# Pool's queue carries the statistics and outputs of a dilated attention, and keys and values of the next pair are loaded in parts

## The chip, the cores and the metric

The kernel runs on one core of one Trainium2 chip. The metric is device time in microseconds (us). It was timed three times before the change, with a median of 3201.4 us. One more execution was profiled, and every row below is of that one.

## What is computed

The reference is a trunk of two decoder layers over 2048 positions of 1024 channels, in float32. The change touches the mixer of the second layer only, a causal dilated attention with three branches of 16 heads:

```
DILATED_CONFIGS = ((128, 1), (512, 4), (2048, 16))
...
def dilated_mixture(q, k, v):
    branches = [dilated_window_branch(q, k, v, d, w // d) for (w, d) in DILATED_CONFIGS]
    big_m = branches[0][1]
    for _, m_i, _ in branches[1:]:
        big_m = jnp.maximum(big_m, m_i)
    num = 0.0
    den = 0.0
    for o_i, m_i, l_i in branches:
        w_i = l_i * jnp.exp(m_i - big_m)
        num = num + w_i * o_i.astype(jnp.float32)
        den = den + w_i
    return (num / den).astype(v.dtype)
```

Each branch has, for every head and query, an output, a row maximum m and a row sum l. The outputs are added with weights made from m and l, then multiplied by a gate, silu of a fourth projection.

## The kernel before

Queries, keys, values and gates of the second layer are written to DRAM by the projections. The function `dilated` reads them back. It handles the 16 heads as eight pairs p = 0 to 7, a pair in four chunks c of 512 queries, and a chunk as four units: a half of the chunk (`half`) in each of two branches `br` (the first two dilations share one). A unit multiplies queries with keys (L1268, tile `s_ps`), adds a mask and takes the row minimum on DVE (L1276), takes the exponential with its row sum on ACT (L1278), transposes the result on PE (`flip`, L709) with copies back from PSUM (L713, tile `pt`), and multiplies with the values (L1309, tile `o_ps`).

What joins the branches is `merge`. Its steps hang behind the last unit of a pair and are issued one per unit while the next pair runs:

- `rows` transposes the statistics of a pair and writes them to DRAM (ACT copy L1337 into `rt`, then four DMAs `std<-rt`).
- `columns` reads them back in another layout (nine DMAs `W<-std`). The first five bring what the first step of `weights` needs, the last four what L1358 needs.
- `weights` makes the weights on DVE (L1355 `mm`, L1356, L1358, L1359 to L1364) and ACT (L1357).
- `expand` spreads them over partitions on Pool (L1370, tile `X`), and `chunk` multiplies each output with its weight (PE L1378, DVE L1379), adds the two branches and multiplies with the gate on Pool (L1385, L1386), and writes the result to DRAM (`og`).

Pairs 0 to 6 merge all four chunks at once (n = 4). Pair 7 merges each chunk by itself, since the output projection that follows waits for it. The projection (`out_proj`, PE L618) loads the outputs back; its first four row tiles and one weight tile are loaded from Pool's queue.

A DMA is issued by the engine whose queue `queue[0]` holds: SP (`nc.sync`) everywhere in `dilated` apart from the first loads, which Pool (`PO`) issues. Each engine runs its instructions in order, and a DMA that waits for a semaphore holds everything behind it in its queue. The order of an engine's instructions is set when the program is built, by a planner that moves an instruction to where it expects it to be ready. A load that is issued early in the code therefore stands in SP's queue behind other loads and waits only for its buffer.

Keys take four buffers (two pairs), values four (two pairs of two branches), queries three, gates four.

Of the kernel before, what the change touches and what calls it, by code (L numbers as in the profile page):

```python
# [8 lines left out]
F32 = mybir.dt.float32  # L9
F32R = mybir.dt.float32r  # L10
# [8 lines left out]
S, D = 2048, 1024  # L19
# [64 lines left out]
def trunk(ctx: ExitStack, tc: tile.TileContext, A, out):  # L84
    nc = tc.nc
    V, SC, PO, TE = nc.vector, nc.scalar, nc.gpsimd, nc.tensor

    queue = [nc.sync]
    QA = PO

    def dma(o, i):
        if o.dtype == F32R:
            o = o.bitcast(F32)
        if i.dtype == F32R:
            i = i.bitcast(F32)
        return queue[0].dma_start(o, i)  # L96
# [7 lines left out]
    def dap(t, off, ap):  # L104
        return bass.AP(tensor=t.tensor, offset=t.offset + off, ap=ap)

    def pool(es, name, bufs=1, space=None, side=None):
        kw = {"space": space} if space is not None else {}
        if side is not None:
            kw["side"] = side  # L110
        return es.enter_context(tc.tile_pool(name=name, bufs=bufs, reuse_waits="tile", **kw))
# [6 lines left out]
    k1 = dram.tile([2, 16, 64, S], F32R, name="k1")  # L118
    v_d = [dram.tile([S, 1024], F32, name=f"v_{l}") for l in range(2)]
    sg_d = [dram.tile([8, 128, S], F32, name=f"sg_{l}") for l in range(2)]  # L120
# [448 lines left out]
    for u in range(4):  # L569
# [3 lines left out]
                 lambda part, j, c, u=u: qk0[2 * u + j][part, :, 512 * c:512 * c + 512])  # L573
# [30 lines left out]
    def split_wo(raw, where):  # L604

        for c in (0, 512):
            hi, lo = where[:, c:c + 512], where[:, D + c:D + c + 512]
            SC.copy(hi, raw[:, c:c + 512])
            V.tensor_tensor(lo, raw[:, c:c + 512], hi.bitcast(F32), OP.subtract)
# [536 lines left out]
    def dilated():  # L1146
        es = ExitStack()
        kp = pool(wo_es, "kp1")
        ap = pool(es, "dl")
        ap2 = pool(es, "dl2")  # L1150
# [3 lines left out]
        wo = []  # L1154
        keys, queries, values, gates, stats, outs, Os, raws = {}, {}, {}, {}, {}, {}, {}, []

        def load_k(p, cuts=(0, 1024, 2048)):

            keys[p] = K = [kp.tile([128, S], F32R, tag="K", name="K", bufs=4) for _ in range(2)]
            for a, b in zip(cuts[:-1], cuts[1:]):  # L1160
                for k in range(2):
                    dma(K[k][:, a:b], dap(k1, (16 * k + 2 * p) * 64 * S + a, [[S, 128], [1, b - a]]))

        def load_q(p, c, parts=(0, 4)):

            queries[p, c] = Q = kp.tile([128, 4, 512], F32R, tag="Q", name="Q", bufs=3)
            for a, b in zip(parts[:-1], parts[1:]):
                dma(Q[:, a:b], dap(q1, (128 * p * 16 + 4 * c + a) * 512, [[16 * 512, 128], [512, b - a], [1, 512]]))
# [13 lines left out]
        band = kp.tile([128, 768], F32, name="band")  # L1182
        bands = band[:, 0:512], band[:, 512:768]
        queue[0] = QA
        load_k(0, (0, 512))
        load_q(0, 0, (0, 2, 4))
        dma(band, A["cst"][:, C_MB:C_MB + 768])
        for k in range(2):
# [46 lines left out]
        def unit(p, c, br, half):  # L1235
# [6 lines left out]
            def start():  # L1242
                if half == 0 and br == 0:
                    g = 4 * p + c + 1
                    if g < 32:
                        load_q(g // 4, g % 4)
                    if c == 0:
                        stats[p] = ap.tile([128, 4, 2, 2, 2, 4], F32, tag="st", name="st", bufs=2)
                        if p < 7:
                            load_k(p + 1)  # L1250

            def scores(js):
                Kh, Kl = keys[p]
# [29 lines left out]
            def turn(s):  # L1283
                if s == 0:
                    if p == 7 and br == 0 and c > 0:
                        (out_weights if half == 0 else lambda e: split_wo(raws[e // 2][:, e % 2], wo[e]))(c - 1)
                    if p < 7 and (c, half) == (1, 0):
                        load_v(p + 1, br)
                engs = []
                for _ in range(2):  # L1290
                    count[0] += 1
                    engs.append(SC if count[0] % 3 == 0 else V)
                where.update(zip(steps[s], flip(ap, aps, [box["P"][:, hh, j, o:o + 128] for hh, j, o, kc in steps[s]],
                                                engs, DPT_BUFS)))
# [30 lines left out]
        def merge(p, c0, n):  # L1325

            box = {}
            R = 8 * n
            sd = st_d[p + c0]

            def rows():

                ps = x_bank("x_ps")
                TE.transpose(ps[0:4 * R, 0:128],
                             stats[p][:, c0:c0 + n].rearrange("p c x b h t -> p (c x b h t)"), ident)
                rt = ap2.tile([128, 128], F32, tag="rt", name="rt", bufs=2)
                SC.copy(rt[0:4 * R], ps[0:4 * R, 0:128])  # L1337
                for c in range(n):
                    dma(dap(sd, c * 512, [[n * 512, 8], [128, 4], [1, 128]]), rt[32 * c:32 * c + 32])

            def columns():

                box["W"] = W = ap2.tile([128, 2, 2, 128], F32, tag="W", name="W", bufs=1)
                dma(W[0:R, :, 0], dap(sd, 0, [[128, R], [2 * R * 128, 2], [1, 128]]))
                for k in range(2):
                    for t in range(4):
                        dma(W[0:R, k, 1, 32 * t:32 * t + 32],
                            dap(sd, (2 * k + 1) * R * 128 + 128 * t, [[512, 2 * n], [32, 4], [1, 32]]))

            def weights():  # L1350
                W = box["W"][0:R]
                m, l = W[:, 0], W[:, 1]
                mm = ap2.tile([128, 128], F32, tag="mm", name="mm", bufs=1)[0:R]
                E = ap2.tile([128, 2, 128], F32, tag="E", name="E", bufs=1)[0:R]
                V.tensor_tensor(mm, m[:, 0], m[:, 1], OP.min)  # L1355
                V.tensor_tensor(E, mm[:, None, :].to_broadcast([R, 2, 128]), m, OP.subtract)  # L1356
                SC.activation(E, E, AF.Exp)  # L1357
                V.tensor_tensor(l, l, E, OP.mult)  # L1358
                V.tensor_tensor(mm, l[:, 0], l[:, 1], OP.add)  # L1359
                V.reciprocal(mm, mm)  # L1360
                V.tensor_tensor(E, E, mm[:, None, :].to_broadcast([R, 2, 128]), OP.mult)
                ws = [ap2.tile([128, 2, 128], F32R, tag=f"w{k}", name=f"w{k}", bufs=1)[0:R] for k in range(2)]
                V.tensor_copy(ws[0], E)
                V.tensor_tensor(ws[1], E, ws[0].bitcast(F32), OP.subtract)  # L1364
                box["w"] = ws

            def expand(br):

                for k in range(2):
                    PO.tensor_tensor(X[64 * br + 32 * k:64 * br + 32 * k + R].rearrange("p (r y) -> p r y", r=4),  # L1370
                                     box["w"][k][:, br, None, :].bitcast(F32).to_broadcast([R, 4, 128]),
                                     cc[0:R, C_M4:C_M4 + 4, None].to_broadcast([R, 4, 128]), OP.mult)

            def chunk(c, br):
                o = outs[p, br, c]
                bc = x_bank("bc_ps")
                bs = slice(64 * br, 64 * br + 64)
                TE.matmul(bc, sels[2 + c if n == 4 else 6][bs], X[bs], start=True, stop=True)  # L1378
                V.tensor_tensor(o, bc, o, OP.mult)  # L1379
                if br == 0:  # L1380
                    gates[p, c] = ap2.tile([128, 512], F32, tag="sg", name="sg", bufs=4)
                    dma(gates[p, c], sg_d[1][p, :, 512 * c:512 * c + 512])
                    return
                eng = V if (p, c) == (7, 3) else PO
                eng.tensor_tensor(o, o, outs[p, 0, c], OP.add)  # L1385
                eng.tensor_tensor(o, o, gates[p, c], OP.mult)  # L1386
                dma(og_d[1][c][p], o)

            if p < 6:
                fs = [rows, columns, None, None, weights, lambda: expand(0), lambda: expand(1), None]  # L1390
                fs += [lambda c=c, br=br: chunk(c, br) for c in range(4) for br in range(2)]
            else:
                fs = [rows, columns] + [None] * (c0 < 3) + [weights, lambda: (expand(0), expand(1))]
                fs += [lambda c=c: (chunk(c, 0), chunk(c, 1)) for c in range(c0, c0 + n)]
            return [(i + 1, f) for i, f in enumerate(fs) if f]
# [16 lines left out]
    DLEAD, DPT_BUFS, OR_BUFS = 4, 6, 11  # L1412
    wo_es = ExitStack()
    wo_tiles = dilated()

    out_proj(1, None, *wo_tiles)
# [51 lines left out]
```

## Time and profile before

| what | value |
|---|---|
| three timed executions | 3199.12, 3201.4, 3201.77 us |
| the profiled execution, its own time | 3197.35 us |
| its span, first to last instruction | 3195.4 us |
| PE busy | 3052.8 us (96%) |
| DVE, ACT, Pool busy | 1567.6, 1281.4, 511.2 us |
| mean granted TensorE clock | 0.976 |
| bytes moved by DMA | 415.27 MB, 130 GB/s |

The profiled execution is 1.95 us longer than its span, and 4.05 us under the median. The dilated attention runs from about 2499 us to about 2997 us of the span, with the output projection behind it. A busy time is the time in which an engine had an instruction under way; a matmul at half clock is busy for twice as long. The granted clock is a share of 2.4 GHz.

### The profile page before, as it was taken

What the parts mean: (1) busy time and instruction counts of PE and PEld (TensorE: products, weight loads), DVE (VectorE), ACT (ScalarE), POOL (GpSimd) and SP (SyncE); (2) the same over time, 40 slices, a digit from 0 to 9 for tenths busy, and PEclk for the clock granted to TensorE, in tenths of its full rate; (3) what the DMA queues carried; (4) which work ended last, traced back from release to release, by engine and by line L of the source; (5) the groups of instructions that cost most, each with busy time, mean ns of one, the idle gap of its engine ahead of it and who ended that gap; (6) DMA issues with size and microseconds to landing.
All of it is one profiled execution on the core that took longest, in us unless ns stands there. A gap on an engine that the chain in (4) does not pass through costs nothing. (4 is left out here: it accounts for less than half of the span.)

```text
span 3195.4 us, 60888 instructions
## 1 busy us (share of the span) xinstructions
PE 3052.8 (96%) x24252; PEld 2498.1 (78%) x24252; DVE 1567.6 (49%) x4176; ACT 1281.4 (40%) x2954; POOL 511.2 (16%) x495
## 2 busy tenths in 40 slices
PE   7999999999999999999999999999999988988898
PEld 5978888987777777677778999888888777777687
DVE  6443421000777778888654411411100578878643
ACT  4411111111766665655542221111111677776321
POOL 3200100001332310000033101320000012213321
PEclk8999999999999999999999999999999999998899
DMA  7255553215323222222253323675322755654252
GB/s 256 74 189 194 156 154 104 73 61 183 111 92 118 82 68 74 73 69 67 80 187 107 126 81 118 205 216 157 115 82 94 214 165 180 196 167 146 91 175 97
DMA packets 272309, 415.27 MB, mean 130 GB/s; under 512 B 28172, under 2 KB 155788, under 8 KB 267032
## 3 DMA queue, kind: packets, MB, share of 16 engines
q1 hardware_dynamic: 268712, 399.58, 38.9%
q0 software_dynamic: 3312, 11.80, 1.2%
q8 instruction: 190, 3.11, 0.4%
q14 instruction: 95, 0.78, 0.1%
HBM read 259.23 MB, written 152.05 MB: 129 GB/s over the span
## 5 line engine op out<-in xcount | busy, mean ns | idle before, releaser
L246 PE MATMUL pj<-hl,wh 128*128 128x512 f32 x1536 | 389.6, 396 | 0.0
L246 PE MATMUL pj<-hh,wh 128*128 128x512 f32 x1536 | 389.3, 395 | 0.0
L246 PE MATMUL pj<-hh,wl 128*128 128x512 f32 x1536 | 388.3, 395 | 0.0
L834 PE MATMUL s_ps<-K,Q 64*128 64x512 f32 (+2 forms) x1920 | 335.5, 392 | 19.1 <-DVE P L843 15.1
L246 PEld LDWEIGHTS pj<-hl,wh 128*128 128x128 f32 x1536 | 289.1, 188 | 68.6 <-issue 0.2
L854 ACT ACTIVATE P<-P,m 128x1664 f32<-128x1664 f32 (+15 forms) x256 | 306.7, 1200 | 88.0 <-DVE m L849 87.8
L246 PEld LDWEIGHTS pj<-hh,wl 128*128 128x128 f32 x1536 | 288.5, 188 | 68.3 <-issue 0.2
L246 PEld LDWEIGHTS pj<-hh,wh 128*128 128x128 f32 x1536 | 288.2, 188 | 68.4 <-issue 1.0
L709 PE MATMUL t_ps<-cc,P 64*128 64x64 f32 x5536 | 306.4, 234 | 29.5 <-DVE pt L713 19.1
L709 PEld LDWEIGHTS t_ps<-cc,P 64*128 64x128 f32 x5536 | 239.9, 142 | 107.5 <-issue 57.2
L923 PEld LDWEIGHTS o_ps<-pt,v 128*64 128x64 f32 (+1 forms) x3264 | 248.9, 156 | 85.8 <-issue 52.3
L923 PE MATMUL o_ps<-pt,v 128*64 128x128 f32 (+1 forms) x3264 | 311.9, 284 | 2.9 <-ACT pt L713 2.7
L1278 ACT ACTIVATE P<-P,st 128x256 f32<-128x256 f32 (+3 forms) x512 | 267.0, 524 | 89.5 <-DVE st L1276 88.2
L231 DVE TENSOR_TENSOR wl<-w,wh 128x512 fp32r<-128x512 f32 (+1 forms) x128 | 84.8, 705 | 406.7 <-ACT wh L230 406.7
L713 ACT COPY pt<-t_ps 128x512 f32<-128x512 f32 (+7 forms) x448 | 213.5, 496 | 164.7 <-PE t_ps L709 152.2
L713 DVE COPY pt<-t_ps 128x512 f32<-128x512 f32 (+5 forms) x384 | 229.6, 608 | 75.7 <-PE t_ps L709 64.2
L1276 DVE CUSTOM_DVE_ANT_0 P<-s_ps,band 128x256 f32<-128x256 f32 (+3 forms) x512 | 204.4, 446 | 98.6 <-PE s_ps L1268 95.3
L834 PEld LDWEIGHTS s_ps<-K,Q 64*128 64x128 f32 x1920 | 200.5, 191 | 61.1 <-DVE P L843 25.3
L1268 PE MATMUL s_ps<-K,Q 64*128 64x256 f32 (+2 forms) x1536 | 192.4, 337 | 24.7 <-DVE st L1276 23.6
L267 ACT ACTIVATE hi<-pj 128x512 fp32r<-128x512 f32 x80 | 47.9, 599 | 348.8 <-PE pj L246 327.7
L268 DVE SCALAR_TENSOR_TENSOR lo<-pj,hi 128x512 fp32r<-128x512 f32 x80 | 55.2, 690 | 246.0 <-ACT hi L267 233.8
L840 DVE CUSTOM_DVE_ANT_0 P<-s_ps,F 128x512 f32<-128x512 f32 (+1 forms) x192 | 121.4, 670 | 109.9 <-PE s_ps L834 109.1
(245 smaller groups left out, 4475.5 us busy)
## 6 DMA issues: line engine op xcount, KB each, us to landing
Q<-q SPq DMA_DIRECT2D x31, 1024.0 KB
ada<-ada_w SPq DMA_DIRECT2D x96, 256.0 KB
sg<-t2k SPq DMA_DIRECT2D x64, 256.0 KB
xt<-x SPq DMA_DIRECT2D x32, 512.0 KB
w<-w SPq DMA_DIRECT2D x64, 256.0 KB
q<-yb SPq DMA_DIRECT2D x64, 256.0 KB
x<-x SPq DMA_DIRECT2D x28, 512.0 KB
w<-w0b SPq DMA_DIRECT2D x56, 256.0 KB
```

The costliest lines, as they stand in the source:

```text
L231: V.tensor_tensor(wl[:, 2 * q:2 * q + 2, :n], w[:, :, :n], wh[:, 2 * q:2 * q + 2, :n].bitcast(F32), OP.subtract)
L246: TE.matmul(ps, a[:, d, 128 * j:128 * j + 128], b[:, d, :], start=n == 0, stop=n == 23)
L268: V.scalar_tensor_tensor(lo, src, scale, hi.bitcast(F32), OP.mult, OP.subtract)
L709: TE.transpose(ps[k][:, n], b[rs], ident[rs, rs])
L713: last_flip[eng is SC] = f(pt[:, :len(blocks), 64 * k:64 * k + 64], ps[k][:, :len(blocks)])
L834: TE.matmul(ps[j][:, :n], queries[p, i // 4][hs, a, qs], keys[p][b][hs, c0:c0 + n], start=first, stop=a == 1)
L840: V.tensor_tensor_reduce(P[:, c0:c0 + n], ps[j][:, :n], forgets[p][j][:, c0:c0 + n], 1.0, 3.0e38, OP.add, OP.min, m)
L854: SC.activation(P, P, AF.Exp, bias=lows[j], scale=-1.0, accum_out=lt[:, j, col:col + 1])
L923: TE.matmul(o[:, cs], values[p][:, b, hs], pts[j, b], start=b == 0, stop=b == i)
L1268: TE.matmul(ps[hh][:, o:o + N], q[hs, qs], t["keys"](kk[hs]), start=k == 0, stop=k == 2)
L1276: V.tensor_tensor_reduce(P[:, hh, j, :n], ps[hh][:, o:o + n], m[:, m.shape[1] - n:], 1.0, 3.0e38, OP.add, OP.min, mn)
L1278: SC.activation(P[:, hh, j, :n], P[:, hh, j, :n], AF.Exp, bias=mn, scale=-1.0, accum_out=l)
```

## The change

Four things are edited. `rows` issues its writes, `columns` its reads, and `chunk` its output write from Pool's queue (the output of the last chunk of pair 7, which DVE computes, stays with SP). The four gate loads of a merge move from `chunk` to `rows`. The keys of the next pair are loaded as two parts, one at the start of chunk 1 and one at chunk 2, where both were loaded at chunk 0. The values of the next pair are loaded at chunk 3, one branch in each half, where both were loaded at the first half of chunk 1.

```
-        def load_k(p, cuts=(0, 1024, 2048)):
+        def load_k(p, part, cuts=(0, 1024, 2048)):
...
-            keys[p] = K = [kp.tile([128, S], F32R, tag="K", name="K", bufs=4) for _ in range(2)]
+            K = kp.tile([128, S], F32R, tag="K", name="K", bufs=4)
+            keys[p] = keys.get(p, []) + [K]
...
                     if c == 0:
                         stats[p] = ap.tile([128, 4, 2, 2, 2, 4], F32, tag="st", name="st", bufs=2)
-                        if p < 7:
-                            load_k(p + 1)
+                    if c in (1, 2) and p < 7:
+                        load_k(p + 1, c - 1)
...
-                    if p < 7 and (c, half) == (1, 0):
+                    if p < 7 and (c, half) == (3, br):
                         load_v(p + 1, br)
...
+                queue[0] = PO
                 for c in range(n):
                     dma(dap(sd, c * 512, [[n * 512, 8], [128, 4], [1, 128]]), rt[32 * c:32 * c + 32])
+                queue[0] = nc.sync
+                for c in range(c0, c0 + n):
+                    gates[p, c] = ap2.tile([128, 512], F32, tag="sg", name="sg", bufs=4)
+                    dma(gates[p, c], sg_d[1][p, :, 512 * c:512 * c + 512])
...
             def columns():
 
+                queue[0] = PO
                 box["W"] = W = ap2.tile([128, 2, 2, 128], F32, tag="W", name="W", bufs=1)
...
+                queue[0] = nc.sync
...
                 if br == 0:
-                    gates[p, c] = ap2.tile([128, 512], F32, tag="sg", name="sg", bufs=4)
-                    dma(gates[p, c], sg_d[1][p, :, 512 * c:512 * c + 512])
                     return
...
+                queue[0] = nc.sync if eng is V else PO
                 dma(og_d[1][c][p], o)
+                queue[0] = nc.sync
```

In SP's queue, around the boundary from one pair to the next, this stands before. `sg<-sg` is a gate load of 256 KB, `og_3` an output, `v` of 128x16x128 a whole branch of values (1 MB), `v` of 32x4x128 a sixteenth of the other branch, `K` 512 KB and `Q` 1 MB.

```order
L96 DMA og_3_79<-or 128x512
L96 DMA v<-v_69 128x16x128
L96 DMA std_90<-rt 8x4x128 x4
L96 DMA v<-v_69 32x4x128 x3
L96 DMA W<-std_90 32x2x128
L96 DMA W<-std_90 32x1x32 x8
L96 DMA v<-v_69 32x4x128 x13
L96 DMA Q<-q_66 128x2048
```

The same place of SP's queue after the change, over one pair:

```order
L96 DMA sg<-sg_71 128x512 x2
L96 DMA K<-k_67 128x1024
L96 DMA Q<-q_66 128x2048
L96 DMA K<-k_67 128x1024
L96 DMA sg<-sg_71 128x512
L96 DMA K<-k_67 128x1024 x2
L96 DMA Q<-q_66 128x2048
L96 DMA sg<-sg_71 128x512
L96 DMA v<-v_69 128x16x128
L96 DMA v<-v_69 32x4x128 x8
L96 DMA Q<-q_66 128x2048
L96 DMA v<-v_69 32x4x128 x8
```

The statistics and the output are gone from it; the values still stand in one row behind the last gate load of a merge, split only by a query load.

Pool's queue at the same boundary before. `X` is `expand` of a merge, the `or` lines are the additions and gate products of its chunks.

```order
L1385 TENSOR_TENSOR or<-or 128x512
L1386 TENSOR_TENSOR or<-or,sg 128x512
L1370 TENSOR_TENSOR X<-w_28935,cc 32x512 x2
L1370 TENSOR_TENSOR X<-w_28936,cc 32x512 x2
L1385 TENSOR_TENSOR or<-or 128x512
```

Pool's queue at the same place after (its lines 1391, 1392 and 1378 are lines 1385, 1386 and 1370 of before):

```order
L1391 TENSOR_TENSOR or<-or 128x512
L1392 TENSOR_TENSOR or<-or,sg 128x512
L96 DMA og_3_79<-or 128x512
L96 DMA std_91<-rt 8x4x128 x4
L96 DMA W<-std_91 32x2x128
L96 DMA W<-std_91 32x1x32 x8
L1378 TENSOR_TENSOR X<-w_28940,cc 32x512 x2
L1378 TENSOR_TENSOR X<-w_28941,cc 32x512 x2
```

Thirteen DMAs of statistics now stand between the last output of one merge and the `X` of the next.

At the end of the attention, the last merge (pair 7, chunk 3) before, in Pool's queue:

```order
L1370 TENSOR_TENSOR X<-w_32841,cc 8x512 x2
L1370 TENSOR_TENSOR X<-w_32842,cc 8x512 x2
L1385 TENSOR_TENSOR or<-or 128x512
L1386 TENSOR_TENSOR or<-or,sg 128x512
L1370 TENSOR_TENSOR X<-w_32991,cc 8x512 x2
L1370 TENSOR_TENSOR X<-w_32992,cc 8x512 x2
```

And after:

```order
L1378 TENSOR_TENSOR X<-w_32843,cc 8x512 x2
L1378 TENSOR_TENSOR X<-w_32844,cc 8x512 x2
L96 DMA W<-std_98 8x2x128
L96 DMA W<-std_98 8x1x32 x4
L1391 TENSOR_TENSOR or<-or 128x512
L96 DMA W<-std_98 8x1x32
L1392 TENSOR_TENSOR or<-or,sg 128x512
L96 DMA W<-std_98 8x1x32
L96 DMA og_2_78<-or 128x512
L96 DMA W<-std_98 8x1x32 x2
L1378 TENSOR_TENSOR X<-w_32993,cc 8x512 x2
L1378 TENSOR_TENSOR X<-w_32994,cc 8x512 x2
```

The nine reads of the last merge's statistics stand behind the `X` of the merge before and between that merge's additions.

## Rows read from the trace of the kernel before

**Rows 1.** Waits of DVE, 2560 to 2900 us: total, times, longest.

```profile
DVE mm L1355 <- DMA W<-std: 24.1, 6, 6.4
DVE W L1358 <- DMA W<-std: 5.6, 5, 1.3
```

**Rows 2.** Waits of PE, 2560 to 2900 us, the whole answer.

```profile
PE s_ps L1268 <- DVE st L1276: 18.8, 30, 2.0
PE t_ps L709 <- DVE pt L713: 18.4, 6, 5.2
PE t_ps L709 <- ACT pt L713: 1.1, 2, 0.5
```

**Rows 3.** Timeline of the fifth boundary: start us, us, what, [idle before, releaser].

```profile
2797.96 0.26 ACT L1337 COPY rt<-x_ps 128x128 f32<-128x128 f32 x1
...
2798.25 3.80 SPq L96 DMA_DIRECT2D std<-rt  x4
...
2802.15 1.33 SPq L96 DMA_DIRECT2D v<-v  x3
...
2806.15 6.20 SPq L96 DMA_DIRECT2D W<-std  x9
...
2810.92 0.28 DVE L1355 TENSOR_TENSOR mm<-W 32x128 f32<-32x128 f32 x1 [6.38 <-DMA W<-std]
...
2812.67 1.01 PE L709 MATMUL t_ps<-cc,P 64*128 64x64 f32 x14 [5.24 <-DVE pt L713]
...
2813.89 0.41 DVE L1358 TENSOR_TENSOR W<-W,E 32x256 f32<-32x256 f32 x1 [1.27 <-DMA W<-std]
```

**Rows 4.** Timeline of the first boundary, the same steps.

```profile
2562.80 0.26 ACT L1337 COPY rt<-x_ps 128x128 f32<-128x128 f32 x1
...
2572.34 0.28 DVE L1355 TENSOR_TENSOR mm<-W 32x128 f32<-32x128 f32 x1 [2.17 <-DMA W<-std]
```

**Rows 5.** Windows at six boundaries: us, busy PE, PEld, DVE, ACT, POOL, clock.

```profile
2568.00:2588.00 20.00, 16.46 (x185) 12.84 (x181) 14.53 (x44) 11.93 (x37) 4.23 (x4) 0.74 0.34 103
...
sum 120.00, PE 91.13 PEld 72.75 DVE 84.24 ACT 71.66 POOL 25.31; mean PE 15.19 PEld 12.13 DVE 14.04 ACT 11.94 POOL 4.22
```

**Rows 6.** Windows: six of 20 us later in the same pairs.

```profile
2600.00:2620.00 20.00, 19.47 (x321) 16.75 (x317) 17.58 (x67) 16.08 (x57) 7.13 (x6) 1.00 0.73 239
...
sum 120.00, PE 114.17 PEld 98.08 DVE 100.42 ACT 97.84 POOL 38.03; mean PE 19.03 PEld 16.35 DVE 16.74 ACT 16.31 POOL 6.34
```

**Rows 7.** Windows: all of the six boundaries in one stretch.

```profile
2560.00:2900.00 340.00, 301.54 (x4399) 249.01 (x4395) 278.17 (x975) 256.91 (x864) 81.65 (x68) 0.93 0.56 175
```

**Rows 8.** Timeline of Pool, 2440 to 2460 us: its own DMA issues.

```profile
2454.45 2.16 POOL L96 DMA_DIRECT2D K<-k  x4
```

**Rows 9.** DMA view, 2440 to 2443 us: KB, us from issue to landing.

```profile
K<-k POOLq DMA_DIRECT2D x1, 256.0 KB, 3.3
```

**Rows 10.** DMA view, 3022 to 3022.5 us.

```profile
raw<-od_w_out POOLq DMA_DIRECT2D x1, 512.0 KB, 4.3
```

**Rows 11.** Pool's instructions by line, 2490 to 3034 us: busy, mean ns.

```profile
L1385 POOL TENSOR_TENSOR or<-or 128x512 f32<-128x512 f32 x31 | 39.8, 1283 | 145.4 <-DVE or L1379 142.8 <-issue 2.6
L96 POOL DMA_DIRECT2D ogt<-og x2 | 1.8, 902 | 0.0
```

**Rows 12.** Timeline of Pool, 2942 to 3023 us, around pair 7's merges.

```profile
2942.06 1.28 POOL L1385 TENSOR_TENSOR or<-or 128x512 f32<-128x512 f32 x1 [1.72 <-DVE or L1379]
...
2957.29 4.44 POOL L1370 TENSOR_TENSOR X<-w,cc 8x512 fp32r<-8x512 f32 x4 [1.57 <-PE s_ps L1268]
...
3002.85 4.61 POOL L1370 TENSOR_TENSOR X<-w,cc 8x512 fp32r<-8x512 f32 x4 [11.18 <-DVE w L1363]
```

**Rows 13.** Waits of PE, 2935 to 3035 us.

```profile
PE bc_ps L1378 <- POOL X L1370: 12.4, 7, 3.3
```

**Rows 14.** The chain that ended last: start us, us, what.

```profile
3013.20 1.75 DMA W<-std
...
3033.02 153.55 PE y_ps L618 x676
```

More of the change, by code (lines that the diff above doesn't have):

```diff
@@ L1155, in dilated @@
         keys, queries, values, gates, stats, outs, Os, raws = {}, {}, {}, {}, {}, {}, {}, []
-        def load_k(p, cuts=(0, 1024, 2048)):
-            keys[p] = K = [kp.tile([128, S], F32R, tag="K", name="K", bufs=4) for _ in range(2)]
+        def load_k(p, part, cuts=(0, 1024, 2048)):
+            K = kp.tile([128, S], F32R, tag="K", name="K", bufs=4)
+            keys[p] = keys.get(p, []) + [K]
             for a, b in zip(cuts[:-1], cuts[1:]):
-                for k in range(2):
-                    dma(K[k][:, a:b], dap(k1, (16 * k + 2 * p) * 64 * S + a, [[S, 128], [1, b - a]]))
+                dma(K[:, a:b], dap(k1, (16 * part + 2 * p) * 64 * S + a, [[S, 128], [1, b - a]]))
         def load_q(p, c, parts=(0, 4)):
@@ L1184, in dilated @@
         queue[0] = QA
-        load_k(0, (0, 512))
+        for k in range(2):
+            load_k(0, k, (0, 512))
         load_q(0, 0, (0, 2, 4))
```

## The prediction

> **What bounds the kernel now.** PE is busy for almost the whole span, so I looked for the places where it is not, in the part that the change touches. The first view is the list of waits of the six boundaries at which pairs 0 to 5 are merged, 2560 to 2900 us. DVE waits 24.1 us in six waits for the statistics to come back (`mm`, the first step of `weights`) and another 5.6 us in five for their second half [rows 1]. PE's list for the same time is short: 18.4 us in six waits for `pt` copies of DVE, and 18.8 us in thirty for DVE's minimum [rows 2]. No row of it names keys, queries or values: the loads of those come in time, and moving them can give PE nothing directly.
>
> The second view is the timeline of the fifth boundary, the worst [rows 3]. `rt` is done at 2798.22. SP issues the four writes until 2802.05, then three loads of values that stand in between, then waits for the writes to land, and starts the nine reads at 2806.15. `mm` starts at 2810.92, 12.70 us after `rt`; DVE had been ready 6.38 us earlier, 6.3 us after `rt`. Behind `mm` in DVE's queue stand the minima and copies that PE needs, so PE stops for 5.24 us. At the first boundary `mm` starts 9.28 us after `rt`, and DVE was ready at 7.1 us [rows 4]. So DVE is ready some 6.7 us after `rt`, and the round trip through DRAM takes 9.3 to 12.7 us: by the mean wait of 4.0 us, 10.7.
>
> The third view gives the whole price. In six stretches of 20 us at these boundaries PE is busy for 91.1 of 120 us [rows 5], in six later in the same pairs for 114.2 [rows 6]: 23 us more of idle time. The granted clock falls as well: over 2560 to 2900 it is 0.93 [rows 7], and since the low level is half of the high one, 2 x 0.07 x 340 = 48 us of it, some 8 at each boundary, ran at 1.2 GHz. Of these 8, about 4 are idle anyway and 4 do work in twice the time, 2 us lost each. The six boundaries thus cost about 23 + 12 = 35 us, the most that the change could win there.
>
> **The change part by part.** *Issue on Pool.* Pool has issued plain loads here at 0.55 us each, four in 2.16 us [rows 8]; one with eight pieces a partition took 0.90 [rows 11]. The statistics are small DMAs of 32 or 64 pieces; I take 0.55 and keep 0.9 as the upper end. A landing on Pool's queue took 3.3 us for 256 KB [rows 9] and 4.3 us for 512 KB [rows 10]; 1.0 us for 256 KB more leaves an estimate of 2.3 us for almost nothing. SP's last read of 8 rows landed 1.75 us after its issue [rows 14], so 1.75 is the lower end. A write among the 1 MB of values that are in flight will land later. In the one queue of now the reads were held for 4.1 us behind the last write (2802.05 to 2806.15 [rows 3]), 2.4 more than 1.75: that is the upper end. On a queue where no values stand ahead of it I take 0.5.
>
> The round trip at a boundary is then: 0.25 for two hand-overs, 3 x 0.55 until the fourth write is issued, 2.8 until it lands, 4 x 0.55 until the fifth read is issued, 2.3 until it lands. That is 9.2 us, against 10.7. DVE's wait falls from 4.0 to 2.5. The ninth read lands at 0.25 + 1.65 + 2.8 + 8 x 0.55 + 2.3 = 11.4; DVE reaches L1358 1.7 us after `mm` (2813.89 less the wait of 1.27, less 2810.92 [rows 3]), here at 10.9, which leaves 0.5 of the present 1.1 us. PE's idle time follows DVE's: 18.4 us of PE for 24.1 of DVE [rows 1, 2], or 0.76; for the second wait I take 1. A boundary saves 1.5 x 0.76 + 0.6 = 1.7 us, six save 10.4.
>
> *Clock.* At the first boundary DVE waits least, 2.17 us [rows 4], and its stretch has the clock 0.74 [rows 5], no better than the mean. A shorter wait need not bring the clock back. I take 3 of the 12 us as saved, between none and all.
>
> *Loads in parts.* SP runs its queue as far ahead as buffers allow. The last gate load of a merge waits for Pool's product of the merge before, and the values of the next pair stand right behind it, as they stood behind the output `og_3`. So they still start just ahead of the statistics, and what the edit takes away is that the statistics stand behind them in the same queue. Keys and queries are not waited for now [rows 2] and keep most of a pair of lead: nothing. The gates come earlier, by SP, behind no wait of PE: nothing. If that cover fails, the values of the second branch are late next, and PE would wait at `o_ps`.
>
> *Outputs on Pool.* Four issues of 0.55 us in a pair on an engine that is busy for 81.65 of 340 us [rows 7]: hidden until the last pair.
>
> *The end.* There Pool is not free. Between the first addition at 2942.06 and the `X` at 2957.29 are 15.2 us, of which eight operations of 1.28 us fill 10.3 [rows 11, 12]. The change puts nine reads and four outputs into the other 4.9 us: 13 x 0.55 = 7.2. `X` starts 2.3 us later, and PE waits for it (7 waits for `X`, 12.4 us, now [rows 13]). The third merge of that pair loses an estimated 0.3 us, since its reads land 0.55 us later at most. The last: `X` ends at 3007.46 [rows 12], five reads follow until 3010.2, then two additions of 1.3 with two reads, the output and the last two reads. The ninth is issued at 3015.05 and lands at 3017.35, where it landed at 3013.20 + 1.75 = 3014.95 [rows 14]: 2.4 us later, and the output projection, which runs without a gap from 3033.02 to the end [rows 14], starts that much later. Sum 5.0 us lost.
>
> *Sum.* 10.4 + 3 - 5 = 8.4 us gained: 3197.35 - 8.4 = 3189 for an execution like the profiled one. That one lies 4.05 us under the median, so the forecast of the median is 3201.4 - 8.4 = **3193 us**.
>
> The Trainium skill, "DMA: Bandwidth & Descriptors", section "Queues, rings and completion order", says that a DMA engine takes turns between the queues that have work for it, a packet at a time. The rows show one queue only, in which the writes stand behind values [rows 3], and no run here shows two busy ones yet. By that rule the writes would pass nearly all of the values and the sum would stay as it is; without it they would cost the 2.4 us, and the time would be that of the second rival.
>
> **The rivals.** *The stall goes.* If the round trip takes under 7 us, DVE does not wait. That takes landings of 1.75 us and no traffic: 0.25 + 1.65 + 1.75 + 2.2 + 1.75 = 7.6, still 0.9 over. PE's pause would be some 0.7 us. In the quiet stretches it idles 1.0 us in each 20 with the clock at 1.00 [rows 6], so most of the 35 us would come back: 30 less 5 gives 3176. For it: such short pauses cost no clock there. Against it: it needs the lowest price everywhere.
>
> *Nothing moves.* The values still arrive with the statistics. If their traffic holds Pool's writes as it held SP's, a write costs up to 1.9 us more than I assume and the round trip is 10.7 to 11.1 as before. Then the first wait saves nothing, the second 0.6 us at most at each boundary, 3.6 in all, and the end loses 5: 3201.4 + 1.4 to 3201.4 + 5, so 3203 to 3206.
>
> *Slower, by Pool's price.* SP needs 6.20 / 9 = 0.69 us for one of these reads [rows 3], more than Pool's 0.55 for plain loads [rows 8]. If the shape costs Pool as much or more, the gain goes: each 0.1 us adds 0.7 us to the first wait and 0.4 to the second, 5.6 us over six boundaries, and some 2 at the end. From 0.66 us on the change is a loss. At 0.9 us it is 0.35 x 76 = 27 us worse than the forecast: 3220. For it: SP's own price; against it: all of Pool's one-piece loads agree at 0.55.
>
> The Trainium skill, "SBUF — State Buffer", section "SBUF: two separate sides", warns that a DMA issued from Pool cannot write its descriptors while DVE holds the port that both share, in its faster modes. As a mechanism of this kernel: DVE is busy for 278 of 340 us [rows 7], so an issue on Pool could have to wait for a DVE instruction, which leads by another way to the price of 0.9 us and to 3220; I give it 0.05 of that rival's chance. Pool's last loads, `ogt` at 0.90 us for eight pieces a partition [rows 11], show no such wait.
>
> **How the numbers follow.** A change of under 0.2% (6.4 us) can hardly be told from none in this kernel. My forecast, a shorter stall that stays, has 0.42; the stall gone 0.15; nothing moves 0.20; slower by Pool's price 0.23. Of the forecast's cases about two thirds gain more than 6.4 us. Faster 0.28 + 0.15 + 0.02 = 0.45; same 0.12 + 0.16 = 0.28; slower 0.02 + 0.02 + 0.23 = 0.27. The range is 3170 to 3216: below lies the deepest part of the second case, above the upper half of the last, about 0.2 together. The forecast's own range is 3186 to 3199.
>
> **What would show it.** Right: `std` and `W` on Pool's queue at 0.55 us an issue; `W` starting 4.5 to 5 us after `rt` (now 7.9 [rows 3]); DVE's waits for `W` near 15 us for `mm` and 3 for L1358; PE's waits for `t_ps` near 11 to 12; the last `X` some 2.5 us later. Wrong: issues over 0.66 us, writes that land no sooner, DVE's wait at or above 24 us, a clock that recovers wholly or falls lower, or a new wait of PE for values at `o_ps`.

## The result, and the profile after the change

The change makes the kernel slower: 3236.2 us median of four runs (3228.64 to 3239.89), against 3200.26 for the kernel before beside it, a ratio of 1.0111 (95% interval 1.0092 to 1.0129). The forecast was 3193 us in a range of 3170 to 3216. The medians differ by 35.9 us. The profiled execution took 3239.89 us, with a span of 3238.1, 42.7 more than the profiled one of before; the accounts below are of these two.

DVE's waits over the same six boundaries, 2563 to 2925 us (total, times, longest), where [rows 1] had 24.1 and 5.6:

```profile
DVE mm L1363 <- DMA W<-std: 56.5, 6, 11.0
DVE or L1387 <- PE bc_ps L1386: 13.2, 16, 1.9
```

The wait for the first five reads has more than doubled, and the one for the last four is gone: they now land during the longer first one. The whole answer for PE, where [rows 2] had 18.8, 18.4 and 1.1:

```profile
PE t_ps L709 <- DVE pt L713: 35.0, 4, 9.8
PE s_ps L1269 <- DVE st L1277: 27.8, 26, 9.6
PE t_ps L709 <- ACT pt L713: 1.1, 2, 0.5
```

PE waits for no other engine than before and for no keys or values. Windows of 20 us at the six boundaries (the first of them, their sum) and the whole stretch; columns as in [rows 5], and the last three are granted clock, DMA share and GB/s:

```profile
2572.00:2592.00 20.00, 13.46 (x173) 10.87 (x171) 12.22 (x37) 9.87 (x33) 9.22 (x13) 0.74 0.31 85
...
sum 120.00, PE 65.94 PEld 53.52 DVE 66.50 ACT 48.60 POOL 54.31; mean PE 10.99 PEld 8.92 DVE 11.08 ACT 8.10 POOL 9.05
```
```profile
2563.00:2925.00 362.00, 297.90 (x4326) 247.15 (x4324) 273.34 (x966) 252.96 (x854) 135.36 (x166) 0.90 0.54 164
```

PE is busy for 65.9 of 120 us, down from 91.1. Over the stretch the clock is 0.90 (0.93 in [rows 7]): 2 x 0.10 x 362 = 72 us at 1.2 GHz, where it was 48.

The fifth boundary, to be laid beside [rows 3]:

```profile
2818.80 9.52 SPq L96 DMA_DIRECT2D v<-v  x8
2820.93 0.26 ACT L1338 COPY rt<-x_ps 128x128 f32<-128x128 f32 x1
2821.48 2.21 POOL L96 DMA_DIRECT2D std<-rt  x4 [3.69 <-ACT rt L1338]
2829.22 0.77 SPq L96 DMA_DIRECT2D Q<-q  x1
2829.56 4.35 POOL L96 DMA_DIRECT2D W<-std  x8 [5.86 <-DMA std<-rt]
2830.04 5.45 SPq L96 DMA_DIRECT2D v<-v  x8
2834.40 0.54 POOL L96 DMA_DIRECT2D W<-std  x1 [0.49 <-DMA W<-std]
2837.37 0.28 DVE L1363 TENSOR_TENSOR mm<-W 32x128 f32<-32x128 f32 x1 [9.83 <-DMA W<-std]
2839.12 1.01 PE L709 MATMUL t_ps<-cc,P 64*128 64x64 f32 x14 [8.68 <-DVE pt L713]
```

`mm` starts 16.2 us after `rt`. Pool issues the four writes in 2.21 us, as forecast, and then waits 5.86 us for them to land. The reads start at 2829.56. In the same moment SP, which nothing holds any more, sends a megabyte of queries and eight pieces of values, and the first five reads need 7.81 us until `mm` can start. In [rows 3] that took 4.77.

What the DMA engines did meanwhile shows the difference best. A slice of the row `DMA` is a fortieth of the window, its digit the busy share in tenths. First before the change, 2798 to 2811 us, the round trip of [rows 3]:

```profile
DMA  9999999965312121445610002000300000000000
```

Then after it, 2821 to 2837 us, with the groups of issues (KB each, median us from issue to landing):

```profile
DMA  9999999999999898879332009579999899999995
...
W<-std POOLq DMA_DIRECT2D x8, 4.0 KB, 5.5
std<-rt POOLq DMA_DIRECT2D x4, 16.0 KB, 6.3
W<-std POOLq DMA_DIRECT2D x1, 32.0 KB, 4.6
```

Before, the engines are full for the first 3 us, and once the three loads of values behind the writes have drained, they are nearly idle while the reads run. After, they are full in both legs.

At the end, the last run of the projection starts at 3074.47 us, where [rows 14] had 3033.02:

```profile
3074.47 155.14 PE y_ps L618 x676
```

So 41.5 of the 42.7 us are lost before it. I split them at the ends of the `rt` copies, with the first and the seventh as marks. **A** is the time between these two, six boundaries with the pairs between them, and **B** the time from the seventh to that run of the projection. A grew from 354.9 to 381.2 us (+26.4), B from 115.1 to 126.8 (+11.7). The other 3.4 lie ahead of the first mark. Single profiles of the kernels below, which differ little up to there, have that mark anywhere from 2559.9 to 2572.2 us, so I compare A and B between kernels, and not the ends.

### The profile page after: what moved, and what is told of

Read it like the earlier page. It is cut to its first block, busy times and chain, and to the rows that moved or that the text cites. A ratio compares the mean times of both kernels' runs of the same rounds, so it can differ in the third digit from the quotient of the medians.

```text
span 3238.1 us, 60926 instructions
## 1 busy us (share of the span) xinstructions
PE 3062.7 (95%) x24252; PEld 2508.6 (77%) x24252; DVE 1572.5 (49%) x4176; ACT 1281.5 (40%) x2954; POOL 601.1 (19%) x657
## 5 line engine op out<-in xcount | busy, mean ns | idle before, releaser
L834 PEld LDWEIGHTS s_ps<-K,Q 64*128 64x128 f32 x1920 | 202.8, 192 | 60.7 <-DVE P L843 24.5
L1269 PEld LDWEIGHTS s_ps<-K,Q 64*128 64x128 f32 x1536 | 142.6, 203 | 54.9 <-DVE st L1277 41.8
```

The source lines that it names most:

```text
L834: TE.matmul(ps[j][:, :n], queries[p, i // 4][hs, a, qs], keys[p][b][hs, c0:c0 + n], start=first, stop=a == 1)
L1269: TE.matmul(ps[hh][:, o:o + N], q[hs, qs], t["keys"](kk[hs]), start=k == 0, stop=k == 2)
```

## The experiments

For each kernel the table gives the **write leg** (end of `rt` to the first read's issue) and the **read leg** (from there to the start of `mm`), means of the six boundaries; DVE's wait for `mm` over them; A and B; and the median with its ratio to the kernel before, timed beside it (its medians were 3200.3 to 3203.7 us). All but the last two columns are of one profiled execution. No read leg is given where `mm` stands so late that it does not wait.

| kernel | write, read leg | wait | A | B | median | ratio (95%) |
|---|---|---|---|---|---|---|
| before | 6.2, 4.5 | 24.1 | 354.9 | 115.1 | | |
| after | 8.6, 7.4 | 56.5 | 381.2 | 126.8 | 3236.2 | 1.0111 (1.0092–1.0129) |
| e1_stats_pool | 8.3, 5.0 | 40.4 | 378.4 | 124.8 | 3232.9 | 1.0099 (1.0080–1.0117) |
| e2_loads_only | 6.6, 4.6 | 24.2 | 360.3 | 115.5 | 3202.1 | 0.9999 (0.9988–1.0011) |
| e3_outputs_pool | 6.1, 4.5 | 23.3 | 352.4 | 112.9 | 3194.6 | 0.9982 (0.9968–0.9996) |
| e4_no_values | 4.7, 5.2 | 19.8 | 348.6 | 129.4 | 3206.0 | 1.0014 (0.9998–1.0031) |
| e5_values_pool | 9.6, 4.6 | 41.5 | 370.7 | 127.2 | 3230.9 | 1.0085 (1.0067–1.0103) |
| e6_reads_sp | 7.7, 4.5 | 33.2 | 362.8 | 115.4 | 3211.0 | 1.0025 (1.0015–1.0035) |
| e7_weights_later | 9.2, 6.7 | 49.1 | 387.4 | 126.1 | 3249.0 | 1.0142 (1.0118–1.0166) |
| e8_before_later | 7.1, 4.7 | 24.2 | 365.1 | 115.9 | 3212.6 | 1.0029 (1.0017–1.0041) |
| e9_values_behind_x | 4.7, 5.5 | 21.7 | 371.8 | 126.2 | 3222.2 | 1.0075 (1.0056–1.0093) |
| e10_before_mm_later | 6.4, – | 0 | 339.3 | 115.9 | 3187.1 | 0.9962 (0.9949–0.9974) |
| e11_after_mm_later | 8.3, – | 0.2 | 345.5 | 125.9 | 3207.6 | 1.0026 (1.0013–1.0040) |
| e12_outputs_pool_mm_later | 5.8, – | 0 | 339.7 | 113.6 | 3184.0 | 0.9951 (0.9936–0.9966) |
| e13_last_pair_sp | 8.6, 7.7 | 58.1 | 382.3 | 116.3 | 3229.1 | 1.0079 (1.0064–1.0094) |
| e14_products_dve | 8.7, 7.4 | 57.2 | 380.2 | 123.1 | 3231.5 | 1.0090 (1.0073–1.0107) |

### Which part: e1 to e3

**e1_stats_pool** is the kernel before with `queue[0] = PO` around the writes and around the reads.

```
+                queue[0] = PO
                 for c in range(n):
                     dma(dap(sd, c * 512, [[n * 512, 8], [128, 4], [1, 128]]), rt[32 * c:32 * c + 32])
+                queue[0] = nc.sync
...
```

> The kernel before with one part of the change: the writes and reads of the statistics go out from Pool's queue; loads and outputs stay as they were. Theory T (traffic): in the kernel before, SP waits for the writes to land and thereby also holds back the values and queries that stand behind them, so the reads meet an idle DMA; with the statistics on Pool nothing holds the loads, and both legs of the round trip share the DMA engines with 2 MB. T expects rt to mm of 15 to 17 us at the six boundaries, DVE's wait for mm 50 to 60 us (24 before), and most of the loss: 3220 to 3236 us. Theory P (Pool's queue lands slowly of itself, whatever else moves) expects the same here. Theory L (the moved loads of keys and values are the loss) expects about 3200 us and a wait near 24 us.

It has nearly the whole loss, so L falls, but T came true only in part: `rt` to `mm` took 13.3 us, not 15 to 17, and the wait for `mm` is 40.4 us, not 50 to 60. The write leg is the slow one (8.3 us, with no outputs on Pool's queue, so these are not what delays the writes). The read leg is not slow, except at the first boundary. At the other five it took 4.5 to 4.9 us, although pieces of values of 64 KB were issued all through it; at the first, where SP issued the query load of 1 MB 1.1 us into the leg, it took 6.8. At the five that load came 2.8 to 4.0 us into the leg, and the last two reads took 4.1 to 5.6 us to land. So the loss stands in both of DVE's waits, which over 2563 to 2925 us add up to 56.1, nearly the 56.5 after the change:

```profile
DVE mm L1359 <- DMA W<-std: 40.4, 6, 7.6
DVE W L1362 <- DMA W<-std: 15.7, 5, 3.7
```

**e2_loads_only** is the changed kernel without its `queue[0] = PO` lines.

> The changed kernel with statistics and outputs put back on SP's queue, so that only the loads of keys, values and gates are moved. T and P expect a wait for mm of 20 to 28 us and 3196 to 3206 us, as before the change. L expects 3220 us or more.

No difference: L falls here too. (Its A is 5.4 us above that of the kernel before at an equal median: a single profile's A can be off by as much.) **e3_outputs_pool** moves `dma(og_d[1][c][p], o)` alone to Pool.

> The kernel before with the outputs alone moved to Pool's queue. T and P expect no difference that can be told: 3196 to 3206 us. A rival, that Pool's outputs at the end of the attention cost PE, would show at pair 7 and give 3208 us or more.

The outputs cost nothing: the median, 3194.6 us, is 1.4 under the range, and by its interval this part gains 0.04 to 0.32%.

### What delays the statistics: e4, e5, e6, e9

**e4_no_values** leaves out the loading of values after the first pair.

```
-                        load_v(p + 1, br)
+                        values[p + 1, br] = values[p, br]
```

> The changed kernel, but pairs 1 to 7 multiply with the values of pair 0, so that their 2 MB a pair are not loaded (its output is another). T expects the writes to land in 1.7 to 3 us after the fourth issue instead of 4 to 7, rt to mm 8 to 11 us instead of 16, DVE's wait for mm below 25 us instead of 56, and 3195 to 3212 us. P expects rt to mm of 14 us or more still, and 3225 us or more.

T holds: the same DMAs on the same queue take 4.7 and 5.2 us, where they took 8.6 and 7.4, and the wait is a third. P falls for the boundaries. B stayed high, which led to e13.

**e5_values_pool** puts `queue[0] = PO` around `load_v(p + 1, br)`.

> The changed kernel with the values of the next pair loaded from Pool's queue at chunk 3, behind the merge's outputs, so that nothing is left out and they cannot run ahead to the boundary. T (values and queries in flight delay both legs) expects rt to mm of 9 to 11 us, as without values, DVE's wait for mm below 28 us (56 after the change), and 3195 to 3210 us; 17 more issues of 0.55 us a pair on Pool lie beside other work. A rival, that it was not where the values move but that they moved at all on SP beside the statistics (the number of queues), expects the same wait as after the change, 3230 us or more.

T's number was missed, because the kernel did not do what I meant. Chunk 3 of one pair lies next to the boundary, and Pool had the values at the very place that I wanted to clear: at the fourth boundary it issues four loads of values from 2752.93 on, `std` from 2756.50 on, and further values around `W`. The write leg is the longest of the table; the read leg, with no values from SP beside it, fell to 4.6. The time, 3230.9 us, is that of the rival, but the wait, 41.5 us and not 56, is not; this run decides nothing between the two, and e9 does.

**e6_reads_sp** drops the two `queue[0]` lines of `columns`: the writes stay on Pool, the reads go back to SP.

> The changed kernel with the nine reads back on SP's queue, the four writes still on Pool's. The reads then wait in SP's queue and hold the queries and most of the values back. T expects the write leg as after the change (landing 6 to 8.6 us after rt), but the read leg short: the fifth read lands some 2 us after its issue, not 4 to 6, rt to mm 12.5 to 14.5 us instead of 16, and 3212 to 3228 us. If the writes alone were the loss, rt to mm would stay at 16 and the time at 3236.

The read leg is 4.5 us again, and the write leg still 7.7. The fifth boundary:

```profile
2813.10 2.21 POOL L96 DMA_DIRECT2D std<-rt  x4 [3.69 <-ACT rt L1338]
2820.76 5.87 SPq L96 DMA_DIRECT2D W<-std  x9
2825.24 0.28 DVE L1361 TENSOR_TENSOR mm<-W 32x128 f32<-32x128 f32 x1 [6.12 <-DMA W<-std]
2826.73 0.38 SPq L96 DMA_DIRECT2D Q<-q  x1
```

The queries now leave after the reads, since SP stood at its wait for the writes. The round trip of 12.1 us and the time of 3211.0 lie just under the ranges named; for the time, B went back to 115.4 as well, which I had not counted.

**e9_values_behind_x** mends e5: the values go out from Pool behind the `X` of the running merge, some 20 us after the statistics.

```
-                        load_v(p + 1, br)
+                        if p == 0:
+                            load_v(p + 1, br)
+                        else:
+                            queue[0] = PO
+                            with tc.issue_after(last_flip["X"].ins):
+                                load_v(p + 1, br)
+                            queue[0] = nc.sync
...
```

The values of pair 1, for which no merge runs yet, stay with SP.

> The changed kernel with the values loaded from Pool's queue and tied behind the X of the merge, which stands 20 us after the statistics, so that no values move at the boundary and nothing is left out. In the run with values on Pool at chunk 3 they had still stood right ahead of the writes in Pool's queue, so that run did not separate them. T (values in flight delay both legs) expects rt to mm of 9 to 11 us as in the run without values, DVE's wait for mm near 25 us and a time of 3200 to 3215 us. If the round trip stays over 14 us and the time over 3228, the values are not what delays the statistics on Pool's queue.

Round trip and wait came as T expected (10.2 and 21.7 us), with every value loaded, on the same queue that had the writes at 8.6 us. At the fifth boundary, 2817 to 2830 us, the writes land in 1.8 us, not 6.3; the queries still come in the read leg (the second full stretch):

```profile
DMA  9996731101010100092679989986400010010000
...
W<-std POOLq DMA_DIRECT2D x8, 4.0 KB, 3.8
std<-rt POOLq DMA_DIRECT2D x4, 16.0 KB, 1.8
```

The time did not follow to 3215, since the edit made a wait of its own. PE's waits, 2565 to 2925 us:

```profile
PE s_ps L1269 <- DVE st L1277: 18.4, 26, 3.5
PE o_ps L1316 <- ACT or L1319: 16.8, 6, 4.0
PE t_ps L709 <- DVE pt L713: 10.3, 4, 3.1
```

The loads on Pool hold its additions back, these hold the `or` buffers, ACT's copy waits for one, and PE for ACT: 16.8 us that are not there before.

### Does all of it go through DVE's wait: e7, e8, e10 to e12

**e7_weights_later** and **e8_before_later** put two empty steps ahead of `weights`, in the changed kernel and in the kernel before.

```
-                fs = [rows, columns, None, None, weights, lambda: expand(0), lambda: expand(1), None]
+                fs = [rows, columns, None, None, None, None, weights, lambda: expand(0), lambda: expand(1), None]
```

> The changed kernel, but weights and all that follows it in a merge is put two steps later in pairs 0 to 5. If DVE's wait for mm is what the six boundaries lose, two steps (some 5 us of DVE's work) take 25 to 40 of its 56 us away and the time falls to 3205 to 3218 us. If instead the loads themselves or the clock are the loss, the time stays above 3228.

> The kernel before with the same two steps of delay. By the same reasoning its wait of 24 us for mm goes to under 5, PE's waits for pt in these stretches with it, and the time falls by 12 to 30 us to 3172 to 3190 us. If PE only meets the same wait at another place (the additions of the merge now collide with later units), it stays at 3200.

Both missed, and say nothing of the wait (nor, though e7's time lies above 3228, of the loads or the clock), since the planner moved `mm` forward again: in the built program it stands one minimum further back at the first boundary of e8, and the wait is still 24.2. What did move is the rest of the merge, which now runs into the next boundary: DVE's waits for `bc_ps` rose from 13.7 us to 28.0.

**e10_before_mm_later** ties `weights` behind the copies of DVE that are issued up to step 9 (`weights` stood at step 5), and issues the first chunks two at a time so that the merge ends in its old place. **e11_after_mm_later** does it in the changed kernel at step 10.

```
+            def held():
+                with tc.issue_after(last_flip[False].ins):
+                    weights()
...
-                fs = [rows, columns, None, None, weights, lambda: expand(0), lambda: expand(1), None]
+                fs = [rows, columns] + [None] * 6 + [held, lambda: (expand(0), expand(1))]
...
```

> The kernel before with mm tied behind the copies of later units in DVE's queue, 13 to 21 instructions further back at the boundaries, with the outputs' steps doubled up so that the merge ends where it ended. The earlier attempt at two steps of delay had moved mm by one minimum only, which is why the wait had stayed at 24 us. If the wait is what the boundaries lose, it falls below 6 us, PE's 18 us of waits for pt with it, and the time to 3172 to 3190 us. If PE's time does not follow, the loss at the boundaries is not the wait and the time stays within 3196 to 3206 us.

> The changed kernel with mm 19 to 27 instructions further back at the boundaries. If all that the slower round trip does goes through this wait (56 us after the change), the wait falls to 5 to 20 us and the time to 3196 to 3212 us, with the loss at the last two pairs left over. If the moved traffic also costs in other ways, the time stays above 3220 us.

Both times came as expected; e11's wait fell further than the 5 to 20 us named. In e11 the round trip is as slow as after the change (write leg 8.3 us), yet A falls to 345.5, under that of the kernel before, and the wait is nearly gone (2570 to 2900 us):

```profile
DVE mm L1363 <- DMA W<-std: 0.2, 1, 0.2
```

So at the boundaries the slow round trip costs for the most part through `mm`'s place in DVE's queue: with `mm` moved back in both kernels, A differs by 6.2 us (345.5 in e11, 339.3 in e10), where it differed by 26.4. What the 6.2 are stays open. They are hardly more than the 5.4 by which A was off in e2; the granted clock over A is 0.95 in e11 and 0.98 in e10. In e10 the clock of the stretch is 0.98, where [rows 7] had 0.93:

```profile
2560.00:2900.00 340.00, 311.34 (x4627) 254.78 (x4625) 291.01 (x1029) 268.15 (x909) 86.61 (x72) 0.98 0.58 183
```

PE's waits in e10 (2560 to 2890 us): the one for `pt`, 18.4 us in [rows 2], is nearly gone, and a new one, for ACT's copies into `or`, has come in:

```profile
PE o_ps L1309 <- ACT or L1312: 7.0, 6, 1.6
PE t_ps L709 <- DVE pt L713: 2.8, 6, 0.8
```

**e12_outputs_pool_mm_later** is e3 with the edit of e10.

> The kernel before with only the outputs on Pool's queue (the part that gained 0.18% alone) and mm 13 to 21 instructions further back. If both gains stand beside each other: 3166 to 3186 us, faster than both kernels.

It is faster than both kernels: 3184.0 us, 0.5% under the kernel before. Its interval overlaps that of e10, so that the outputs add a gain to e10's is not shown.

### The end: e13, e14

**e13_last_pair_sp** leaves pair 7's own statistics with SP.

```
-                queue[0] = PO
+                queue[0] = PO if n == 4 else nc.sync
...
```

The same line is put into `rows` and into `columns`.

> The changed kernel with only the statistics of pair 7 (the four merges of one chunk) back on SP's queue. If these reads on Pool make the loss of the end, the time from the last boundary to the projection falls from 126.8 to 113 to 117 us, no DVE instruction there is stretched to 5 us, and the time falls by about 11 us to 3222 to 3228 us. If the loss of the end comes from pair 6 or the outputs, it stays at 124 us or more and the time at 3234 to 3238.

B falls by 10.5 us to 116.3; the median, 3229.1, came 1 us over the range. **e14_products_dve** takes pair 7's additions and products off Pool.

```
-                eng = V if (p, c) == (7, 3) else PO
+                eng = V if p == 7 else PO
...
-                queue[0] = nc.sync if eng is V else PO
+                queue[0] = nc.sync if (p, c) == (7, 3) else PO
```

> The changed kernel with the additions and gate products of pair 7 done by DVE instead of Pool, all DMAs as in the changed kernel. If the products that pile up behind Pool's reads, and the DVE instruction that waits beside them, are the larger part of the loss at the end, the last boundary to the projection takes 114 to 120 us, with no DVE instruction of 5 us, and the whole 3222 to 3231 us. If the reads are simply late, it stays at 123 us or more and the time at 3233 to 3240.

B fell by 3.7 only, and the time, 3231.5, lies between the two ranges. The long DVE instruction stayed (5.17 us): the four products beside it are pair 6's, which this edit does not touch. So the question of how much of B the pile-up on Pool makes is not settled by it.

## Why the prediction was wrong

**Where the stall is, and what moving loads does: right.** The wait for `mm` is the loss at the boundaries; 26.8 us more of DVE's two waits (56.5 against 29.7) go with 26.4 us more of A. Keys, values and gates in parts were put at nothing, and e2 measures 0.9999. The price of the stall was put too high: of the 35 us that the six boundaries were to cost, e10, which takes the whole wait away, gets 15.6 in A and 13.3 in the median, with the new wait of PE shown above.

**The issue on Pool: right.** 0.55 us was forecast. Pool's groups between 2499 and 3075 us show 0.56 to 0.57:

```profile
L96 POOL DMA_DIRECT2D W<-std x99 | 54.0, 568 | 48.2 <-DMA std<-rt 34.8 <-DMA W<-std 8.2 <-DVE pt L713 4.7
L96 POOL DMA_DIRECT2D std<-rt x32 | 17.7, 558 | 100.4 <-ACT rt L1338 90.9 <-DVE or L1387 6.8 <-issue 2.8
```

The rival that ended on the slow side, Pool's price, thus had the right sign for a wrong reason.

**The failed step** is the landing among other traffic: "A write among the 1 MB of values that are in flight will land later [...] On a queue where no values stand ahead of it I take 0.5." The write leg was to take 4.7 us and took 8.6, the read leg 4.5 and took 7.4: 6.8 us too little in a round trip forecast at 9.2. Without values in flight (e9) the write leg takes just the 4.7. The upper end that I gave, 2.4 us for a write, came from the 4.1 us hold in [rows 3], read as the price of sharing a queue. That hold was also a shelter. While SP waited for the writes, it issued no queries and no further values, and the reads met idle DMA engines. The change took the statistics, and with them that wait, out of the queue; e6 puts the reads, and so SP's wait, back, and has the old read leg.

In the read leg it is mainly the queries that the wait had kept off: pieces of values alone left it at 4.5 to 4.9 us (e1), while in e9, with no values there, it took 4.1 and 4.6 us where the queries were issued 1.6 us or more ahead of it and 5.3 to 6.5 where they were issued 0.4 to 0.7 us ahead. With both it took 6.3 to 8.5. No run leaves out the queries alone. For the same reason the rival "nothing moves" was priced too low: it let the other traffic cost a write at most 1.9 us and a read nothing.

The Trainium skill, "DMA: Bandwidth & Descriptors", section "Queues, rings and completion order", has a DMA engine take turns between its queues by packets, and I wrote that by that rule the writes would pass nearly all of the values. They did not: in the trace's packet records of the fifth boundary the first write packet starts 3.4 us after the first issue, 1.2 us in e9. Of the 3072 packets of 512 bytes in which 1.5 MB of values move between 2821.6 and 2830.1 us, about half had started before the first write packet, and over three quarters before the last. The records do not tell by what rule turns are taken; they show that here short writes on a queue of their own did not get ahead of most of the stream.

**The clock** was to give 3 us back and fell instead, from 0.93 to 0.90, with the longer pauses.

**The end** was mis-sized: 5.0 us forecast, 11.7 measured, 10.5 of them from pair 7's statistics (e13). I had counted issues and later landings, but not what Pool's products do to DVE when they pile up behind nine reads (below). How the 11.7 divide between late reads and that pile-up stays open.

**The outputs** were put at nothing and gain a little by themselves. The 3.4 us ahead of the first boundary lie within the spread of single profiles; I leave them open.

## What to carry to other kernels

A wait in a DMA queue also holds back what stands behind it, and may be what keeps bulk loads off a latency-bound round trip; before you move short transfers to a queue of their own, look at the DMA share beside them, and ask what the old queue will send in that time. Where an engine waits for a round trip in the middle of its queue, move the consumer back first (here 0.4% for a few lines, and e12 0.5%), and make sure in the built order that it has moved.

## What the runs showed of the hardware

One DVE instruction on 8 partitions, which takes 0.28 us in the median, took 5.29 us (tail of the kernel after, 2983 to 2990 us):

```profile
2983.57 5.29 DVE L1363 TENSOR_TENSOR mm<-W 8x128 f32<-8x128 f32 x1
2983.72 2.57 POOL L1391 TENSOR_TENSOR or<-or 128x512 f32<-128x512 f32 x2
2986.18 2.53 POOL L1392 TENSOR_TENSOR or<-or,sg 128x512 f32<-128x512 f32 x2
2988.60 1.17 POOL L96 DMA_DIRECT2D og<-or  x2
2989.52 0.69 PE L1269 MATMUL s_ps<-K,Q 64*128 64x384 f32 x1 [4.48 <-DVE or L1387]
```

It ends just behind four operations of Pool, which had piled up behind nine reads and ran without a gap; DVE's next work is late, and PE loses 4.48 us. The other seven kernels with pair 7's reads on Pool show the same: an `mm` or `E` of 5.0 to 5.3 us that ends 0.15 to 0.30 us after the fourth operation. None of the kernels with them on SP has an instruction of DVE there above 2 us. That Pool's operations hold DVE is read from these ends; no run was made for it alone. The Trainium skill, "SBUF — State Buffer", section "SBUF: two separate sides", states that a DVE operation with two inputs in SBUF and a GpSimd operation that reads SBUF exclude each other. The rows agree, though the record of `mm` starts 0.15 us ahead of Pool's first, and show that DVE did not get in between the four. It does not always wait for all: in e13 an `mm` of 1.64 us ends 0.15 us after one addition of Pool, with the next product already behind it. What decides between the two stays open. In the prediction I had used this section the other way round, for DVE holding up Pool's issues; of that the issues of 0.56 us show nothing.
